# Delta-rule stage of a hybrid layer: the lower parts of its weights from GpSimd to VectorE

## The chip, the cores and the metric

The kernel runs on one core of a Trainium2 chip. Its engines are called by short names as the profile has them: PE is TensorE (matmuls; PEld its weight loads), DVE is VectorE, ACT is ScalarE, POOL is GpSimd, and SP is SyncE, which here only issues transfers. Each engine works through its own queue in order and waits on semaphores for the others. The metric is the device time of one execution in microseconds, given as the median of several runs.

## The reference, cut to what matters

One layer of a streaming encoder over 1024 positions and 1024 channels, in float32. One projection of the modulated input feeds two branches, a gated delta rule with 8 heads and a chunked band attention with 16; both are merged by gates, projected, normalised, and a convolved feed-forward part follows.

```python
h = x * (1.0 + scale_t) + shift_t
proj = h @ w_in[l]
qkv_a, z_a, beta_raw, a_raw, q_b, k_b, v_b, gates = jnp.split(proj, IN_SPLITS, axis=-1)
o_a = gated_deltanet(qkv_a, z_a, beta_raw, a_raw, conv_a[l], a_log[l], dt_bias[l], norm_a[l])
o_b = chunk_band_attention(...)
merged = gate_a * (o_a @ w_branch_a[l]) + gate_b * (o_b @ w_branch_b[l])
x = layernorm(DEEPNORM_ALPHA * x + gate_t * (merged @ w_o[l]), ln1_g[l], ln1_b[l])
...
x = layernorm(DEEPNORM_ALPHA * x + gate_f * ffn, ln2_g[l], ln2_b[l])
```

The delta rule of a head: q, k and v go through a causal convolution of width 4 and SiLU; for each chunk a lower triangular system is solved, and a state of 128x128 is carried from chunk to chunk.

## The kernel before, in words

**Split products.** Every large product of float32 matrices is done in three matmuls of a shorter format (fp32r). An operand `a` is split into a high part `ah`, its rounded copy, and a low part `al = a - ah`; the product is `ah*bh + ah*bl + al*bh`. The helper `split` (lines 175 to 180) makes both: the copy at line 177 (on ACT) or 179, the subtraction at line 180 on the engine `le`. `load_split` (line 182) loads a weight block of 128x1024 into a buffer `raw` through the SP queue (line 185) and splits it; `wblock` (line 274) allots the parts `wh` and `wl` and calls it, with ACT for the copy and POOL for the subtraction unless told otherwise. `raw`, `wh` and `wl` have three buffers each (`RB`, `WB`). `mm_fm` (line 280) does the matmuls of one half of 512 positions: 8 slices of 128 rows, three matmuls for each (line 284). A block is thus 48 matmuls, 16 of each of the three kinds.

**Order of the work.** The program is written stage by stage, head by head, but a planner lays the instructions of all engines out before the run, by a timing model of its own and by priorities (`tc.high_priority`), and only the order on each engine comes out of it. So the weight loads run some blocks ahead of their matmuls, and the dense products (TensorE's bulk) are placed between the small, dependent steps of the delta rule.

**The delta-rule stage** takes from about 80 to 800 us. For each of 8 heads there are:
- `stage_k`, `stage_q`, `stage_vz`: the projections of k, q, v and of the output gate z, one weight block each, fetched through the generator `halves` (line 511). `conv_in` (line 520) does the convolution of the projection: a first tap on ACT (line 526), three more on DVE (line 530, 0.74 us each), a tail of three columns added on DVE (line 540, both inputs in SBUF), then SiLU on ACT (line 541). `stage_k` ends with a product of 128x1024 on POOL (line 610), `stage_q` with another (line 636). `pk`, `pq` and `pv` are transposes of k, q and v on TensorE.
- `gate_block` (line 793): a block of the merge gates (`pgt`), also through `halves` (the first gate block, and k and q of head 0, take the products of the first blocks below instead); sixteen of these and two blocks of the attention's keys and queries (those that `EP` lists, through `qk_block`) serve as dense filling.
- `stage_solve` (line 656): 31 steps one after the other, each a product (line 663, both inputs in SBUF) and a reduce (line 665) on DVE; its result goes through DRAM (`ft_d`, from line 667) and back into the tile `dt_`, a part of group G.
- `stage_inverse`: starts with a transpose on DVE (line 682) and the product `pxt` on TensorE (line 687), then small steps over ACT, DVE, POOL and TensorE.
- `stage_chain` (line 716): eight steps of the state; in each, TensorE, DVE (`vs`, line 726, and the state, line 740), ACT (line 732) and TensorE take turns.
- `stage_out`, and `mod_rows` (line 803), which loads rows of another weight into `raw` buffers and sums them on DVE.

Three first blocks (`first_weights`) and the blocks of the later stages (`late_qk_block`, `qk_proj`, `v_proj`, the branch projections) call `wblock` directly, not through `halves`. In the tables the lower parts show as `wl<-raw,wh` at line 180 on POOL.

Of the kernel before, what the change touches and what calls it, by code (L numbers as in the profile page):

```python
# [12 lines left out]
ALU = mybir.AluOpType  # L13
# [4 lines left out]
P = 128  # L18
S = 1024
D = 1024  # L20
NK = 8
# [132 lines left out]
def hybrid_layer(  # L154
# [7 lines left out]
    PE, DVE, ACT, POOL, SP = nc.tensor, nc.vector, nc.scalar, nc.gpsimd, nc.sync  # L162
# [5 lines left out]
    def dump(key, src):  # L168
        if key in dbg:
            SP.dma_start(dbg[key], src)  # L170

    def f(ap):
        return ap.bitcast(F32)

    def split(h, l, src, he, le):
        if he is ACT:
            ACT.copy(h, src)  # L177
        else:
            he.tensor_copy(h, src)
        return le.tensor_tensor(l, src, f(h), ALU.subtract).ins  # L180

    def load_split(h, l, src, he, le, a=1):

        raw = W.tile([P, 1024], F32, tag="raw", bufs=RB, name=nm("raw"))
        SP.dma_start(raw.rearrange("p (a b) -> p a b", a=a) if a > 1 else raw, src)
        split(h, l, raw, he, le)

    def kview(w, c0, n):
        return w[:, c0:c0 + n].rearrange("(k p) n -> p k n", p=P)

    x2, out2 = x[0], out[0]
    w_ada2, w_in2 = w_ada[0], w_in[0]
# [31 lines left out]
    def nm(s):  # L224
        uid[0] += 1
        return f"{s}_{uid[0]}"
# [34 lines left out]
    def ring(key, shape, dtype=F32):  # L261
        return place(step(key, AT[key]), shape, dtype, key)
# [8 lines left out]
    def dhalf(name):  # L271
        return pbank(name, "d")

    def wblock(src, a, he=ACT, le=POOL):
        wh = W.tile([P, 1024], F32R, tag="wh", bufs=WB, name=nm("wh"))
        wl = W.tile([P, 1024], F32R, tag="wl", bufs=WB, name=nm("wl"))
        load_split(wh, wl, src, he, le, a)
        return (wh.rearrange("p (a b) -> p a b", a=a), wl.rearrange("p (a b) -> p a b", a=a))

    def mm_fm(ps, w, rh, rl, n, ks=range(NK)):  # L280
        wh, wl = w
        for k in ks:
            for a, r in ((wh, rh), (wh, rl), (wl, rh)):
                PE.matmul(ps, a[:, k, :], r[k][:, 512 * n:512 * n + 512],  # L284
                          start=(k == 0 and a is wh and r is rh),
                          stop=(k == NK - 1 and a is wl))
# [107 lines left out]
    for j in range(NK):  # L394
# [7 lines left out]
        for n in range(2):  # L402
            N = slice(512 * n, 512 * n + 512)
            px = pbank(nm("px"), "px")
            for t in range(4):
                tr = PE.transpose(px[:, t * P:t * P + P], xs[j][:, 4 * n + t, :], ident)
            ACT.activation(h32[:, N], px, AF.Identity, bias=cs[:, 0:1], scale=cs[:, 1:2])
            ACT.activation(hh[:, j, N], px, AF.Identity, bias=cs[:, 0:1], scale=cs[:, 1:2])
            POOL.tensor_tensor(hl[:, j, N], h32[:, N], f(hh[:, j, N]), ALU.subtract)
# [19 lines left out]
    for n in range(2):  # L429
        N = slice(512 * n, 512 * n + 512)  # L430
# [79 lines left out]

    def halves(name, col0, ready=None):

        w = None if ready else wblock(kview(w_in2, col0, P), NK)
        for n in range(2):
            ps = ready[n] if ready else dhalf(nm(name))
            if not ready:
                mm_fm(ps, w, hhk, hlk, n)
            yield n, slice(512 * n, 512 * n + 512), ps

    def conv_in(h, m):  # L520
        ti = m * NK + h
        y = big(f"y{m}")
        yf = flat(y)
        tail = sm("tail", 3)
        for n, N, ps in halves("pqkv", ti * P, pend.pop("qkv"[m], None) if h == 0 else None):
            ACT.activation(yf[:, N], ps, AF.Copy, scale=col("conv_a", 3 * 24 + ti))
            for tap in (2, 1, 0):
                d = 3 - tap
                o = yf[:, 512 * n + d:512 * n + 512]
                DVE.scalar_tensor_tensor(o, ps[:, :512 - d], col("conv_a", tap * 24 + ti), o,  # L530
                                         ALU.mult, ALU.add)
            if n == 0:

                DVE.tensor_scalar(tail, ps[:, 509:512], col("conv_a", ti), None, ALU.mult)
                for tap in (1, 2):
                    DVE.scalar_tensor_tensor(tail[:, 0:3 - tap], ps[:, 509 + tap:512],
                                             col("conv_a", tap * 24 + ti), tail[:, 0:3 - tap],
                                             ALU.mult, ALU.add)
            else:
                DVE.tensor_tensor(yf[:, 512:515], yf[:, 512:515], tail, ALU.add)  # L540
            ACT.activation(yf[:, N], yf[:, N], AF.Silu)
        return y
# [95 lines left out]
    def stage_vz(h, c):  # L638

        vT = conv_in(h, 2)  # L640
        if h == 0:
            dump("vT", flat(vT))
        vs = c["vs"] = big("vs")
        for g in range(2):
            pv = mbank("pv")
            for t in range(4):
                PE.transpose(pv[:, t, :], vT[:, 4 * g + t, :], ident)
            for t in range(4):
                u = 4 * g + t
                ACT.activation(vs[:, u, :], pv[:, t, :], AF.Copy, scale=c["bk"][:, u:u + 1])  # L650

        sz = c["sz"] = big("sz")
        for n, N, ps in halves("pz", 3 * D + h * P):
            ACT.activation(flat(sz)[:, N], ps, AF.Silu)
# [121 lines left out]
    def qk_block(i):  # L776

        for n, N, ps in halves("pqk", Q0 + i * P):
            gt_ = ring("gt", [P, 512])
            ACT.copy(gt_, ps)  # L780
            SP.dma_start(qk_d[i][:, N], gt_)
# [50 lines left out]
    def some_gates(n):  # L832
        for _, j in zip(range(n), gates):
            gate_block(j)
# [31 lines left out]
    for t in GE:  # L866
        with tc.issue_after(cs[-1]["steps"][t]):
            some_gates(1)


    def qk_proj(c0, p):
        if (c0 - Q0) // P + p in EP + LP:
            raw = W.tile([P, S], F32, tag="raw", bufs=RB, name=nm("raw"))
            SP.dma_start(raw, qk_d[(c0 - Q0) // P + p])
            for n in range(2):
                yield slice(512 * n, 512 * n + 512), raw[:, 512 * n:512 * n + 512]
            return
        w = wblock(kview(w_in2, c0 + p * P, P), NK)
        halves = []
        for n in range(2):  # L880
            ps = pbank(nm("pqk"), "qkv")
            for k in range(NK):
                for a, r in ((w[0], hh), (w[0], hl), (w[1], hh)):
                    PE.matmul(ps, a[:, k, :], r[:, k, 512 * n:512 * n + 512],
                              start=(k == 0 and a is w[0] and r is hh),
                              stop=(k == NK - 1 and a is w[1]))
            yield slice(512 * n, 512 * n + 512), ps

    def v_proj(g):
        w = [wblock(w_in2[4 * P * i:4 * P * i + 4 * P,  # L890
                          Q0 + 2 * D + 256 * g:Q0 + 2 * D + 256 * g + 256].rearrange(
                              "(k p) n -> p k n", p=P), 4) for i in range(2)]
        vts = [[ring("v", [P, 4, 2, P], F32R) for _ in range(2)] for _ in range(2)]
        for t in range(NT):
            ps = pbank(nm("pv"), "qkv")
            for k in range(NK):
                wh, wl = w[k // 4]
                for r, a in ((hh, wh), (hh, wl), (hl, wh)):
                    PE.matmul(ps[:, 0:256], r[:, k, t * P:t * P + P], a[:, k % 4, :],
                              start=(k == 0 and r is hh and a is wh),  # L900
                              stop=(k == NK - 1 and r is hl))
            for q in range(2):
                dst = vts[q][t // 4][:, t % 4]
                src = ps[:, P * q:P * q + P].rearrange("p (e d) -> p e d", e=2)
                ACT.copy(dst[:, :, 0:64], src)
                DVE.tensor_tensor(dst[:, :, 64:P], src, f(dst[:, :, 0:64]), ALU.subtract)
        return vts
# [127 lines left out]
    for br in range(2):  # L1035
# [4 lines left out]
        for j in range(NK):  # L1040
            w = wblock(kview(wbr[br], j * P, P), NK)
            for n in range(2):
                N = slice(512 * n, 512 * n + 512)
# [235 lines left out]
    for t in range(NT):  # L1279
# [5 lines left out]
        for n in range(2):  # L1285
            N = slice(512 * n, 512 * n + 512)
# [248 lines left out]
    for p in range(18, NP):  # L1535
        pair = []
        for i in range(2):
# [4 lines left out]
            h, l = (ring(o, [P, S], F32R) for o in ("lh", "ll"))  # L1542
# [99 lines left out]
```

## Time and profile before

| | |
|---|---|
| median of 3 runs | 2221.73 us (2216.29 to 2221.82) |
| the profiled execution | 2222.92 us |
| its span from first to last instruction | 2221.2 us |
| PE busy | 2125.3 us, 96% |
| DVE busy | 1555.7 us, 70% |
| ACT busy | 1037.9 us, 47% |
| POOL busy | 588.5 us, 26% |
| mean granted TensorE clock | 0.987 |
| PE, DVE, POOL busy from 80 to 800 us | 690.1, 493.1, 218.1 of 720 us |

How to read the profile's lines: a group of instructions is "line engine operation out<-in shape xcount | busy us, mean ns of one | idle time of the engine just before them, and what ended most of it". In a table of stretches the columns are the stretch, its length, the busy time of PE, PEld, DVE, ACT and POOL with the number of instructions, the granted TensorE clock, and the share and rate of the transfers. A line of waits reads "who, at which line, <- for whom: us in total, times, longest us". A line of a timeline is "start, duration, engine, line, operation, out<-in, shape, count". The names of tiles are those of the place in memory: FT holds the solve's result, G among others its coefficients and `dt_`, SA the state, SM small vectors.

### The profile page before, as it was taken

Reading aid. Unit: us, or ns where it says so; the run is one execution under the profiler, and the core shown is the slowest. Engines: PE = TensorE matmul, PEld = TensorE weight load, DVE = VectorE, ACT = ScalarE, POOL = GpSimd, SP = SyncE. Lnnn points to the kernel's source line nnn. Section 1 sums busy time; section 2 is a strip of 40 time slices with the busy share of each in tenths; the row PEclk is TensorE's granted clock in tenths of the full one; section 3 lists DMA queues with packets and bytes.
Section 4 is the critical chain, followed back from the end, with each engine's and each line's share of the span. In section 5 each row is a group of like instructions: output and inputs, shape, how many; then the busy total and the mean of one; then the engine's idle time right before and its main releaser. Section 6 shows DMA issues by size and latency. Waiting matters only on the chain. (4 is left out here: it accounts for less than half of the span.)

```text
span 2221.2 us, 31629 instructions
## 1 busy us (share of the span) xinstructions
PE 2125.3 (96%) x11469; PEld 1776.9 (80%) x11469; DVE 1555.7 (70%) x3228; ACT 1037.9 (47%) x2216; POOL 588.5 (26%) x544
## 2 busy tenths in 40 slices
PE   6998999999999999999999999999899999999998
PEld 5687787777878787798989788888788878887876
DVE  8567585765667664467676653556998788879897
ACT  4645253434334334467675642235544444445453
POOL 4323232332322232233342522424011000000023
PEclk9999999999999999999999999999999999999999
DMA  9232333423233412211111424342242222253222
GB/s 286 80 112 78 91 94 107 119 74 108 85 91 93 142 36 82 79 57 51 60 55 65 154 91 137 105 152 86 67 161 95 86 76 83 89 209 133 95 95 86
DMA packets 228415, 224.68 MB, mean 101 GB/s; under 512 B 27482, under 2 KB 184595, under 8 KB 228259
## 3 DMA queue, kind: packets, MB, share of 16 engines
q1 hardware_dynamic: 228179, 222.63, 31.6%
q8 instruction: 90, 1.47, 0.3%
q14 instruction: 66, 0.54, 0.1%
q10 hardware_dynamic: 80, 0.03, 0.0%
HBM read 180.63 MB, written 48.28 MB: 103 GB/s over the span
## 5 line engine op out<-in xcount | busy, mean ns | idle before, releaser
L180 POOL TENSOR_TENSOR wl<-raw,wh 128x1024 fp32r<-128x1024 f32 x88 | 212.2, 2413 | 325.4 <-ACT wh L177 303.1
L1193 PE MATMUL pup<-hh,wop 128*128 128x512 f32 x704 | 225.2, 391 | 1.6 <-DVE wop L180 1.6
L1193 PE MATMUL pup<-t,wop 128*128 128x512 f32 x792 | 190.1, 393 | 3.3 <-ACT t L177 2.0
L1193 PEld LDWEIGHTS pup<-t,wop 128*128 128x128 f32 x792 | 148.2, 188 | 38.0 <-ACT t L177 2.4
L1193 PEld LDWEIGHTS pup<-hh,wop 128*128 128x128 f32 x704 | 132.0, 188 | 31.0 <-DVE wop L180 2.0
L177 ACT CAST wh<-raw 128x1024 fp32r<-128x1024 f32 x88 | 92.4, 1050 | 134.6 <-DMA raw<-in_w_in_dram 56.0
L1234 POOL TENSOR_TENSOR cc<-cc,G 128x512 f32<-128x512 f32 x22 | 44.6, 2028 | 375.9 <-DVE G L1216 311.7
L284 PE MATMUL pqkv<-hh,wh 128*128 128x512 f32 x352 | 143.1, 407 | 0.0
L284 PE MATMUL pqkv<-hl,wh 128*128 128x512 f32 x352 | 140.8, 400 | 0.0
L284 PE MATMUL pqkv<-hh,wl 128*128 128x512 f32 x352 | 139.8, 399 | 0.0
L1193 PE MATMUL pup<-hl,wop 128*128 128x512 f32 x352 | 137.5, 391 | 0.0
L663 DVE TENSOR_TENSOR FT<-FT,G 128x16 f32<-128x16 f32 (+30 forms) x248 | 120.9, 488 | 17.6 <-POOL G L608 10.3
L944 POOL TENSOR_SCALAR G<-G,FT 128x640 f32<-128x640 f32 (+4 forms) x103 | 69.9, 681 | 182.3 <-DVE FT L943 160.4
L177 ACT CAST wop<-wr 128x512 fp32r<-128x512 f32 x110 | 65.6, 620 | 99.1 <-DVE wr L1179 65.1
L284 PE MATMUL pgt<-hh,wl 128*128 128x512 f32 x240 | 95.1, 396 | 0.8 <-POOL wl L180 0.8
L284 PE MATMUL pgt<-hh,wh 128*128 128x512 f32 x240 | 95.4, 397 | 0.3 <-DVE tmp L530 0.3
L284 PE MATMUL pgt<-hl,wh 128*128 128x512 f32 x240 | 94.7, 395 | 0.0
L1497 PE MATMUL pdn<-hl 128*128 128x512 f32 x360 | 86.7, 395 | 3.9 <-DVE hl L180 2.4
L180 DVE TENSOR_TENSOR wop<-wr,wop 128x512 fp32r<-128x512 f32 x110 | 80.2, 733 | 13.3 <-ACT wop L177 12.4
L963 DVE TENSOR_TENSOR pl<-pp,ph 128x512 fp32r<-128x512 f32 (+2 forms) x116 | 72.5, 635 | 17.4 <-ACT ph L962 16.6
L1497 PEld LDWEIGHTS pdn<-hl 128*128 128x128 f32 x360 | 68.5, 191 | 19.2 <-DVE hl L180 2.8
L941 ACT ACTIVATE G<-G,FT 128x640 f32<-128x640 f32 (+4 forms) x103 | 71.6, 696 | 19.0 <-DVE FT L936 16.9
(457 smaller groups left out, 6127.8 us busy)
## 6 DMA issues: line engine op xcount, KB each, us to landing
raw<-in_w_in_dram SPq DMA_DIRECT2D x72, 512.0 KB
wr<-in_w_up_dram SPq DMA_DIRECT2D x44, 512.0 KB
raw<-in_w_ada_dram SPq DMA_DIRECT2D x32, 512.0 KB
dr<-g_d SPq DMA_DIRECT2D x18, 512.0 KB
dr<-in_w_down_dram SPq DMA_DIRECT2D x18, 512.0 KB
wa<-in_w_ada_dram SPq DMA_DIRECT2D x32, 256.0 KB
gates_d<-GT SPq DMA_DIRECT2D x32, 256.0 KB
g_d<-G SPq DMA_DIRECT2D x14, 512.0 KB
```

Of the source, the lines that this page charges most:

```text
L177: ACT.copy(h, src)
L180: return le.tensor_tensor(l, src, f(h), ALU.subtract).ins
L284: PE.matmul(ps, a[:, k, :], r[k][:, 512 * n:512 * n + 512], start=(k == 0 and a is wh and r is rh), stop=(k == NK - 1 and a is wl))
L663: DVE.tensor_tensor(pr[:, :, 0:i + 1], ft[:, :, 0:i + 1], fa[:, i:i + 1, 0:i + 1].to_broadcast([P, 8, i + 1]), ALU.mult)
L941: ACT.activation(sb[:, 0:n], sb[:, 0:n], AF.Exp, bias=mx[:, nb - 1:nb], scale=-1.0, accum_out=mx[:, 2:3])
L944: POOL.tensor_scalar(sb[:, 0:n], sb[:, 0:n], mx[:, 3:4], 0.0, ALU.mult, ALU.add)
L963: DVE.tensor_tensor(pl[:, B, :], pp, f(ph[:, B, :]), ALU.subtract)
L1193: PE.matmul(ps, a[:, u, k, :], b[v][k], start=(new and k == 0 and u == 0 and v == 0), stop=(k == 3 and u == 1), skip_group_check=not new)
L1234: self.later(7, lambda: POOL.tensor_tensor(o, o, self.t, ADD))
L1497: PE.matmul(sets[s_][i], a[:, u, i * P:i * P + P], b[:, v, :], start=(new and not seed and j == 0 and u == 0 and v == 0), stop=(j == len(q ...
```

## The change

The generator `halves` asks `wblock` for the subtraction on DVE. `split` gets a branch: where the subtraction is on DVE, the source is 1024 wide and a flag `HS` is set, it is done as two instructions of 512 columns. The flag is set while the program up to the end of the delta-rule stage is written and cleared before the attention, so that later splits of that width on DVE stay whole. Nothing else is edited; the copy stays on ACT.

```diff
+    HS = [True]
+
...
             he.tensor_copy(h, src)
+        if le is DVE and src.shape[1:] == [1024] and HS[0]:
+            for n in range(2):
+                N = slice(512 * n, 512 * n + 512)
+                i = DVE.tensor_tensor(l[:, N], src[:, N], f(h)[:, N], ALU.subtract)
+            return i.ins
         return le.tensor_tensor(l, src, f(h), ALU.subtract).ins
...
     def halves(name, col0, ready=None):
 
-        w = None if ready else wblock(kview(w_in2, col0, P), NK)
+        w = None if ready else wblock(kview(w_in2, col0, P), NK, le=DVE)
...
         with tc.issue_after(cs[-1]["steps"][t]):
             some_gates(1)
 
+    HS[0] = False
```

## The prediction

> **What bounds the kernel now.** I began with the busy table and the table of stretches, cut so that the first stretch shown is the delta-rule stage, and then read who waits for whom on TensorE in it.
>
> ```profile
> PE 2125.3 (96%) x11469; PEld 1776.9 (80%) x11469; DVE 1555.7 (70%) x3228; ACT 1037.9 (47%) x2216; POOL 588.5 (26%) x544
> ...
> 80.00:800.00 720.00, 690.05 (x4066) 568.97 (x4065) 493.12 (x1220) 302.05 (x813) 218.07 (x203) 0.99 0.34 99
> ...
> 165.00:250.00 85.00, 79.16 (x505) 63.40 (x504) 60.09 (x148) 36.64 (x95) 27.94 (x36) 0.96 0.33 93
> ...
> 420.00:505.00 85.00, 78.14 (x476) 64.07 (x475) 56.43 (x135) 28.21 (x87) 24.65 (x26) 0.96 0.36 101
> ```
>
> TensorE is the bound of the whole kernel and of this stage: 690 of 720 us. The change takes no matmul away, so it can touch only the 30 us in which TensorE stands there, and the clock: two stretches of 85 us ran at a mean granted clock of 0.96, which is 0.04 x 85 = 3.4 us each. That ceiling, some 37 us or 1.7%, caps every gain below. What TensorE waits for, stage only:
>
> ```profile
> PE pxt L687 <- DMA G<-ft_d: 9.0, 9, 2.1
> PE pvn L729 <- DVE vs L726: 6.4, 8, 2.6
> PE pv L647 <- ACT pq L547: 3.0, 2, 2.3
> PE pk L572 <- ACT y L541: 2.8, 3, 1.5
> PE pu L735 <- ACT SA L732: 2.6, 5, 1.1
> ...
> PE pv L647 <- ACT tmp L541: 1.0, 1, 1.0
> PE pgt L284 <- POOL wl L180: 0.8, 1, 0.8
> ```
>
> Two things are to be seen. The operation that the change moves, the split wl on POOL, holds TensorE up once, for 0.8 us; so nothing is won by having the lower parts earlier. The largest wait is the first product of the inverse (pxt), which wants ft_d, the result of the row-by-row solve on DVE after its way through DRAM. Whatever shortens or lengthens the solve shows there.
>
> **What is removed.** Blocks whose weights change engine are those of the generator halves. Their number follows from the matmuls, 16 of each kind to a block:
>
> ```profile
> L284 PE MATMUL pqkv<-hh,wl 128*128 128x512 f32 x352 | 139.8, 399 | 0.0
> ...
> L284 PE MATMUL pgt<-hh,wl 128*128 128x512 f32 x240 | 95.1, 396 | 0.8 <-POOL wl L180 0.8
> ...
> L284 PE MATMUL pz<-hh,wl 128*128 128x512 f32 x128 | 51.8, 404 | 0.0
> ...
> L284 PE MATMUL pqk<-hh,wl 128*128 128x512 f32 x64 | 25.2, 393 | 0.0
> ```
>
> That is 22 + 15 + 8, and of the four pqk blocks the two that EP lists go through halves as well: 47. The next rows are what such a split costs POOL, and how it goes into a solve (DVE first, then POOL, the same four microseconds):
>
> ```profile
> L180 POOL TENSOR_TENSOR wl<-raw,wh 128x1024 fp32r<-128x1024 f32 x50 | 120.8, 2418 | 222.8 <-ACT wh L177 201.4 <-PE pgt L284 13.3 <-PE pfirst L284 4.3
> ...
> L636 POOL TENSOR_TENSOR y<-y,tmp 128x1024 f32<-128x1024 f32 x8 | 19.1, 2392 | 17.9 <-PE pq L630 13.8 <-ACT po L547 4.2
> L610 POOL TENSOR_TENSOR tmp<-tmp,SB 128x1024 f32<-128x1024 f32 x8 | 19.0, 2378 | 0.0
> ```
> ```profile
> 132.61 0.20 DVE L663 TENSOR_TENSOR FT<-FT,G 128x40 f32<-128x40 f32 x1
> 132.85 0.20 DVE L665 TENSOR_REDUCE FT<-FT 128x8 f32<-128x40 f32 x1
> 133.08 2.04 DVE L663 TENSOR_TENSOR FT<-FT,G 128x48 f32<-128x48 f32 x1
> 135.16 0.20 DVE L665 TENSOR_REDUCE FT<-FT 128x8 f32<-128x48 f32 x1
> 135.40 2.09 DVE L663 TENSOR_TENSOR FT<-FT,G 128x56 f32<-128x56 f32 x1
> ```
> ```profile
> 132.66 2.40 POOL L180 TENSOR_TENSOR wl<-raw,wh 128x1024 fp32r<-128x1024 f32 x1 [1.38 <-ACT wh L177]
> 135.01 2.40 POOL L636 TENSOR_TENSOR y<-y,tmp 128x1024 f32<-128x1024 f32 x1
> ```
>
> POOL loses 47 x 2.42 = 114 us of work, which by itself is worth nothing: POOL is a quarter busy. But a product of the solve, 0.20 us in the row before, takes 2.04 when it starts inside a POOL split, and ends as that split ends (135.12 and 135.06): it stands 1.84 us. How often, over all solves:
>
> ```profile
> L663 DVE TENSOR_TENSOR FT<-FT,G 128x16 f32<-128x16 f32 (+30 forms) x248 | 120.9, 488 | 17.6 <-POOL G L608 10.3
> ...
> L665 DVE TENSOR_REDUCE FT<-FT 128x8 f32<-128x16 f32 (+30 forms) x248 | 73.2, 295 | 6.9
> ```
>
> Product and reduce run over the same widths and take the same 0.20 us where nothing disturbs them, so the products stood for about 120.9 - 73.2 = 47.7 us. One POOL product of line 636 falls in each of the eight solves (it is issued by the query step just ahead) and takes 2.09 - 0.20 = 1.9 us of that, 15 in all, and stays. The other 32.5 us, 4.1 to a head, are some two splits per solve and go away.
>
> The Trainium skill, SBUF — State Buffer, section "Who interferes with whom", says that a VectorE instruction with two SBUF inputs and a GpSimd instruction that reads SBUF exclude each other for the whole of the instruction that came first. The rows above agree for the solve. By the same rule the new halves, which have two SBUF inputs, would in turn be caught by POOL's lines 636 and 610, which the rows do not show for lack of halves. From the rows' times that catch would be (19.1 + 19.0) / 720 = 5% of 94 halves at some 1.2 us each, 6 us more on DVE and at most one on TensorE: the sum below would be -6 instead of -7. I go by the rows of the next part and leave that microsecond to the range.
>
> **What is added.** DVE gets 94 subtractions of 128x512, both inputs in SBUF. The stage has none; the later stages have both widths on DVE (minimum, median, maximum in ns):
>
> ```profile
> L180 DVE TENSOR_TENSOR wop<-wr,wop x110: 670/683/1619, 1460.7 to 1960.2; 128x512 fp32r<-128x512 f32 x110
> ...
> L180 DVE TENSOR_TENSOR ob<-raw,ob x6: 1216/1224/1226, 1279.4 to 1358.2; 128x1024 fp32r<-128x1024 f32 x6
> ```
>
> At 0.683 us that is 64 us. Two halves cost 1.37 against 1.22 for one whole, 7 us over 47 blocks, for which other work may slip between them. DVE in the stage goes from 493 to 493 - 32.5 + 64 = 525 us or 73%: not a bound. What counts is where the halves fall.
>
> In a solve: the two splits that lay inside now put 2 x 1.37 = 2.7 us, with gaps 2.8, between its steps. The solve ends 4.1 - 2.8 = 1.3 us earlier; 4.1 if the planner sets the halves outside. The nine pxt waits sum to 9.0 us, mean 1.0. A cut of 1.3 removes all but the tails of the longest: I take 6.5 us, with bounds 0 (the planner moves pxt forward by as much) and 9.0.
>
> In the convolutions: line 540 is a DVE addition of two SBUF tiles three columns wide, and ACT's SiLU waits behind it.
>
> ```profile
> L540 DVE TENSOR_TENSOR y<-y,SM x16: 145/153/2381, 83.4 to 772.5; 128x3 f32<-128x3 f32 x16
> ...
> ACT y L541 <- DVE y L540: 39.4, 15, 5.5
> ```
>
> Its median is 0.15 us and its longest 2.38, nearly a whole POOL operation. Of the 2.8 + 1.0 us that TensorE waits behind that SiLU I take 1.5, bounds 0 and 3.8. The clock: the two stretches with 0.96 are those in which TensorE idles most, 5.8 and 6.9 us of 85 (from their rows); with waits cut I take 1.5 of the 6.8 us, bounds 0 and 6.8.
>
> In the chain: halves fill 64 / 720 = 9% of DVE's time. A state update of lines 726 or 740 that comes up finds one running 9 times in 100, with 0.34 us left on average, 0.03 us per update; some hundred updates make 3 us on DVE. TensorE has dense blocks to cover most of it; waits for vs were 6.4 us in all. I take 1.0, bounds 0 and 3.
>
> A new wait: the half stands in DVE's in-order queue until ACT's cast of the same block is done. Behind it stand the solve, the convolution taps and the chain's updates, and behind those ACT and TensorE. POOL stood 201 us for such casts at no cost. The next rows are ACT's waits for raw loads, DVE's own halves in the up-projection, and DVE's and SP's waits around the solve:
>
> ```profile
> ACT wh L177 <- DMA raw<-in_w_in_dram: 43.1, 8, 10.8
> ...
> L180 DVE TENSOR_TENSOR wop<-wr,wop 128x512 fp32r<-128x512 f32 x88 | 64.5, 736 | 8.5 <-ACT wop L177 7.9
> ...
> DVE G L682 <- DMA G<-ft_d: 12.0, 4, 8.1
> ...
> SPq L185 <- POOL wl L180: 95.0, 18, 14.2
> ```
>
> By the up-projection, where 88 halves stood 7.9 us in all for their casts, it is 0.09 us a half, 8 us over 94; by ACT's own waits for raw loads, behind which its casts stand, it is 43. The first is the nearer row, since the planner orders both queues. On TensorE I take 1.5, bounds 0 and 15 (worked out under the rivals). The SP queue waits 95 us for splits to free the raw buffer ahead of the next load; the end of a split moves from cast + 2.4 to cast + 1.4 us plus a place in DVE's queue, so I count nothing there. The cover for all lateness of wl is the ring of three buffers: each block is 48 matmuls, so a split has two blocks of time before its reader; if DVE were late by more than that, every microsecond would show on TensorE.
>
> **Sum.** -6.5 - 1.5 - 1.5 + 1.0 + 1.5 = -7.0 us on the profiled execution, which took 2222.92 us (span 2221.2): 2215.9. The median of the runs, 2221.73, lies 1.2 us under it, so I forecast 2214.7, with 2207 to 2219 if this mechanism decides.
>
> **Rivals.** No change: TensorE is 96% busy, the planner lays out all queues anew with the longer DVE work in its books, and puts pxt and the chain so that the same waits come back in other places. What DVE gains in freed products (32.5 us) is half of what it takes on (64), which speaks for this; that pxt waits in most heads for what the plan cannot know speaks against. It gives 2219 to 2224, say 2221.7. The Trainium skill, Perfetto Trace Analysis, section "Optimizing Scalar/DVE Operations", warns in this sense that moving work between GpSimd and VectorE might not help because they share a read port.
>
> Slower: DVE stands at a half for a late cast. The place is just behind each solve: the raw load is issued in the SP queue behind the ft_d transfers, ACT has waited there eight times, 43.1 us in all. DVE would stand with it, and has stood 12.0 us there anyway for ft_d: 31 us new, on the inverse and the first chain steps. If half reaches TensorE, that is +15, and with half of the gain of 7 left, +12: 2234. It decides from the point where the planner places the halves ahead of the inverse's operations in DVE's queue. Against it: that same planner knows that load and its place.
>
> Not what it says: if the shape test at the new branch fails, each block is one subtraction of 1.22 us; DVE saves 7 us, a solve is held in longer pieces, and I expect about 2216 to 2220, a little short of the forecast.
>
> **Chances.** Forecast 0.45, no change 0.27, slower by the cast 0.23, whole subtractions 0.05, which I count as no change. A measurement of this kernel can tell about 0.3%, 6.7 us, from nothing. Faster by more than that 0.45, within it 0.32, slower 0.23. The range takes in the forecast's bounds and most of the slow rival: 2203 to 2234.
>
> **What would show it.** Right: no product of line 663 over 1 us except one per solve (line 636), its mean near 0.36 us; 94 halves at about 0.69 us on DVE between 80 and 800 us; the pxt waits under 4 us; DVE near 525 us there. Wrong: DVE idle before line 180 for ACT's cast of wh in tens of microseconds, with more waits of TensorE for vs or the inverse; or the same 30 us of TensorE's idle time under other names; or a different time in stages after 800 us, which the edit leaves alone except through the planner's order.

## The result and the profile after

The changed kernel took 2230.48 us (median of its runs, 2222.08 to 2240.98) against 2221.20 for the kernel before, a ratio of 1.0043 [1.0032, 1.0054]: 0.43% or some 9.3 us slower, where 7 us faster had been forecast. Its profiled execution took 2233.22 us (span 2231.5), 10.3 more than that of before. Line numbers are 2 to 8 higher in it: the cast is line 179, the split 187, pxt 694, vs 733.

The row for all engines, from the page, and then the delta-rule stage in the table of stretches:

```profile
PE 2136.4 (96%) x11469; PEld 1782.8 (80%) x11469; DVE 1566.4 (70%) x3275; ACT 1033.0 (46%) x2214; POOL 470.9 (21%) x497
```
```profile
80.00:800.00 720.00, 691.46 (x4015) 567.12 (x4014) 496.19 (x1242) 294.37 (x801) 101.31 (x155) 0.98 0.34 99
```

POOL has lost its work (218 to 101 us in the stage), and DVE has hardly more than before (493 to 496). DVE has 47 instructions more in all, 3228 to 3275, and not 94. The groups of DVE say why, and what became of the solve:

```profile
L670 DVE TENSOR_TENSOR FT<-FT,G 128x16 f32<-128x16 f32 (+30 forms) x248 | 93.3, 376 | 14.8 <-POOL G L615 8.1
...
L672 DVE TENSOR_REDUCE FT<-FT 128x8 f32<-128x16 f32 (+30 forms) x248 | 73.2, 295 | 7.0
...
L187 DVE TENSOR_TENSOR wl<-raw,wh 128x1024 fp32r<-128x1024 f32 x47 | 59.9, 1274 | 46.6 <-ACT wh L179 46.3
```

The 47 blocks are whole subtractions of 128x1024: the branch for halves is never taken, because `src.shape[1:]` is a tuple and a tuple never equals the list `[1024]`. What ran is thus the kernel before with nothing but `le=DVE` in `halves`. And the last column has a wait that the kernel before does not have on this engine: 46.3 us before the split, until ACT's cast of the same block. The waits of the stage, first TensorE's and then those of DVE and ACT (who, at which line, for whom: us, times, longest):

```profile
PE pvn L736 <- DVE vs L733: 8.1, 10, 2.6
PE pu L742 <- ACT SA L739: 5.9, 5, 2.0
PE pk L579 <- ACT y L548: 4.1, 5, 2.0
...
PE pks L732 <- DVE SA L747: 2.0, 2, 1.7
...
PE pxt L694 <- DMA G<-ft_d: 0.7, 2, 0.5
```
```profile
DVE wl L187 <- ACT wh L179: 46.3, 24, 5.0
...
ACT wh L179 <- DMA raw<-in_w_in_dram: 41.7, 8, 7.5
```

The pxt waits are nearly gone (9.0 to 0.7 us), as forecast. In their place the waits of the chain and of SiLU have grown: vs 6.4 to 8.1, SA on ACT 2.6 to 5.9, y 2.8 to 4.1, SA on DVE 0.4 to 2.0. DVE's wait for casts is about as long as ACT's own wait for the raw loads behind which the casts stand. One place shows how they hang together. Behind the solve of the seventh head, DVE, then ACT, TensorE and the SP queue:

```profile
738.98 1.30 DVE L689 STREAM_TRANSPOSE G<-G 128x512 f32<-128x512 f32 x2 [2.44 <-DMA G<-ft_d]
740.21 1.49 DVE L825 SCALAR_TENSOR_TENSOR GT<-raw,csil,GT 128x512 f32<-128x512 f32 x2
743.15 1.23 DVE L187 TENSOR_TENSOR wl<-raw,wh 128x1024 fp32r<-128x1024 f32 x1 [1.44 <-ACT wh L179]
744.29 0.34 DVE L733 SCALAR_TENSOR_TENSOR vs<-pks,SM,vs 128x128 f32<-128x128 f32 x1
744.66 0.29 DVE L697 TENSOR_SCALAR G<-pxt 32x128 f32<-32x128 f32 x1
```
```profile
742.07 1.04 ACT L179 CAST wh<-raw 128x1024 fp32r<-128x1024 f32 x1 [5.87 <-DMA raw<-in_w_in_dram]
```
```profile
740.57 0.38 PE L732 MATMUL pks<-SA,y 128*128 128x128 f32 x2
...
744.78 0.64 PE L736 MATMUL pvn<-vs,am 128*128 128x128 f32 x2 [2.56 <-DVE vs L733]
```
```profile
734.81 2.75 SPq L677 DMA_DIRECT2D G<-ft_d  x4
...
738.11 1.17 SPq L192 DMA_DIRECT2D raw<-in_w_in_dram  x2
```

The raw load of v's block is issued behind the solve's transfers (738.11, behind 734.81). So ACT casts it only at 742.07. DVE's queue has the split of that block between the transposes of the inverse (line 689) and everything that follows. It stands 1.44 us and then works for 1.23; the update vs, ready long before (its product pks ran at 740.57), starts at 744.29, and TensorE has stood 2.56 us. The same stands behind six solves (at 255.0, 353.9, 448.3, 553.4, 648.0 and 743.2 us), with waits of 1.4 to 2.8 us, 13.8 together. Other splits, with waits of their own, lie inside the solves: fourteen in all, with 17.1 us of work and 11.8 us of standing. So a solve gets no shorter by the freed products: the eight took 30.1 us on average before and 30.2 after, that of the seventh head 29.2 us in both profiles (691.6 to 720.7 before, 701.6 to 730.8 after). A solve in the third head:

```profile
324.46 0.29 DVE L670 TENSOR_TENSOR FT<-FT,G 128x128 f32<-128x128 f32 x1
...
326.52 1.22 DVE L187 TENSOR_TENSOR wl<-raw,wh 128x1024 fp32r<-128x1024 f32 x1 [1.77 <-ACT wh L179]
327.67 0.28 DVE L672 TENSOR_REDUCE FT<-FT 128x8 f32<-128x128 f32 x1
```

**Idle time and clock.** Summed over the whole profile from the records of TensorE and of its clock, TensorE stood 80.6 us before and 79.7 after, from its first matmul to its last: no more than before. What grew in these two executions is the time at half clock: 11 windows of together 51.2 us before, 16 of 68.3 us after. Half of what TensorE worked in them is lost, 23.2 and 31.9 us; the 8.7 us between these are most of the 10.3. The mean clocks agree: (0.987 - 0.983) x 2231 = 9 us. Over all executions the clock weighs less. Its mean is 0.9855 in the 22 of the changed kernel, and 0.9866 in 77 of the kernel before on the chips of the experiments: 0.0011 x 2230 = some 2.5 of the 9.3 us. The profiled execution is one of the slower ones. The other 7 us are not in the clock, and the profiled pair doesn't show where they lie. The windows begin where gaps lie. Behind the place shown above:

```profile
740.00:744.00 4.00, 2.22 (x25) 1.47 (x23) 2.52 (x4) 1.21 (x2) 0.96 (x4) 1.00 1.07 303
744.00:748.00 4.00, 3.22 (x35) 2.74 (x36) 1.84 (x6) 0.91 (x5) 0.00 (x0) 0.62 0.60 201
```

The granted clock (third column from the end) falls from 1.00 to 0.62 just as TensorE goes on. In these two executions nearly the same sum of idle time thus cost more clock than before. The gaps are not fewer: 75 of over 0.2 us in both, and 24 before and 26 after of over 1 us.

### The profile page after: what moved, and what is told of

It reads as the page before. It is cut to its first block, busy times and chain, and to the rows that moved or that the text cites. A ratio compares the mean times of both kernels' runs of the same rounds, so it can differ in the third digit from the quotient of the medians.

```text
span 2231.5 us, 31652 instructions
## 1 busy us (share of the span) xinstructions
PE 2136.4 (96%) x11469; PEld 1782.8 (80%) x11469; DVE 1566.4 (70%) x3275; ACT 1033.0 (46%) x2214; POOL 470.9 (21%) x497
## 4 chain that ended last, share of the span: by engine, by line
PE 42%; DVE 6%; issue 2%; ACT 1%; DMA 1%; POOL 1%; DVEq 0%; SPq 0%; ACTq 0%; POOLq 0%
PE pup L1201 17%; PE pbr L1055 8%; PE pwo L1117 4%; PE pdn L1505 4%; PE pqk L892 2%; PE pv L907 2%; PE po L982 2%; PE pp L967 1%; PE ps L941 1%; DVE hl L187 1%; DVE hh L1593 1%; DMA dr<-g_d 0%; DVE hh L1519 0%; ACT hh L1588 0%; PE pn L1316 0%
## 5 line engine op out<-in xcount | busy, mean ns | idle before, releaser
L187 POOL TENSOR_TENSOR wl<-raw,wh 128x1024 fp32r<-128x1024 f32 x41 | 98.4, 2402 | 117.6 <-ACT wh L179 111.7
L670 DVE TENSOR_TENSOR FT<-FT,G 128x16 f32<-128x16 f32 (+30 forms) x248 | 93.3, 376 | 14.8 <-POOL G L615 8.1
L187 DVE TENSOR_TENSOR wl<-raw,wh 128x1024 fp32r<-128x1024 f32 x47 | 59.9, 1274 | 46.6 <-ACT wh L179 46.3
L971 DVE TENSOR_TENSOR pl<-pp,ph 128x512 fp32r<-128x512 f32 (+2 forms) x116 | 72.5, 635 | 17.1 <-ACT ph L970 16.2
```

Source lines behind the costliest of these rows:

```text
L670: DVE.tensor_tensor(pr[:, :, 0:i + 1], ft[:, :, 0:i + 1], fa[:, i:i + 1, 0:i + 1].to_broadcast([P, 8, i + 1]), ALU.mult)
L971: DVE.tensor_tensor(pl[:, B, :], pp, f(ph[:, B, :]), ALU.subtract)
```

## The experiments

The theory to be tested, called A in the expectations: the loss is DVE's wait, in order, for ACT's late casts, above all that of v just behind each solve. The rivals put it on the whole subtractions in place of halves, on the operations of DVE and POOL that catch each other, or on the planner's new order of everything. That last one needs a caution for every run: where blocks change engine or place, the planner lays out all queues anew. In the changed kernel at least 1075 of TensorE's 11469 matmuls stand in another order than before (so many have to be left out of both traces for the rest to agree; this count is given below for the other runs). Two pairs were therefore made in which no other instruction moves. Ratios are to the kernel before on the same chip (medians 2219.9 to 2220.2 us).

**The halves made true.** The shape test mended, so that the change does what its diff says.

```diff
-        if le is DVE and src.shape[1:] == [1024] and HS[0]:
+        if le is DVE and tuple(src.shape[1:]) == (1024,) and HS[0]:
```

> The shape test mended, so that each of the 47 subtractions is really made as two of 128x512 on VectorE (0.68 us each). Theory A (VectorE stands in its in-order queue for a late cast, above all for the v block's, whose raw load is issued behind ft_d): the waits for the cast stay, 40 to 55 us on VectorE, and the time stays slower than before by 6 to 12 us. Rival B (sheer load: every block moved costs its share of the 9 to 10 us): 7 us more work on VectorE, so slower by 10 to 12 us. Rival C (the planner's new order happens to be a worse one, whatever the subtractions do): anything between -5 and +12 us, with gaps of TensorE in other places than in the changed kernel.

2227.51 us, 1.0031 [1.0021, 1.0041]. Still slower, perhaps by a little less: the intervals overlap.

```profile
L180 DVE TENSOR_TENSOR wl<-raw,wh x94: 669/684/3246, 81.8 to 766.4; 128x512 fp32r<-128x512 f32 x94
```
```profile
DVE wl L180 <- ACT wh L177: 41.1, 22, 4.8
```

There are 94 halves of 0.68 us, as the prediction priced them, and the wait for casts stays: 41.1 us. That the halves weren't made explains at most a small part.

**v's blocks back on POOL, the other 39 on DVE; and the reverse.**

```diff
-    def halves(name, col0, ready=None):
+    def halves(name, col0, ready=None, le=DVE):
...
-        w = None if ready else wblock(kview(w_in2, col0, P), NK)
+        w = None if ready else wblock(kview(w_in2, col0, P), NK, le=le)
...
-        for n, N, ps in halves("pqkv", ..., ...):
+        for n, N, ps in halves("pqkv", ..., ..., POOL if m == 2 else DVE):
```

The second kernel has `le=POOL` in the first line and `DVE if m == 2 else POOL` in the last.

> As the changed kernel, but the 8 v blocks (one per head, 7 or 8 loads just behind ft_d) keep their subtraction on GpSimd; 39 stay on VectorE. Theory A: VectorE no longer stands before the inverse and the chain; the gaps of TensorE just behind each solve (five of 1.0 to 2.5 us, with half clock after most) go, and with them 5 to 9 us: within 4 us of the kernel before. Rival B: 39/47 of the loss stays, slower by about 8 us. Rival C: anything.

> The kernel before, with only the 8 v blocks moved to VectorE. Theory A: VectorE stands some 2 us for the cast in most heads, 12 to 20 us in all, TensorE shows gaps behind the solves; slower by 4 to 9 us although only a sixth of the blocks is moved. Rival B: a sixth of the loss, slower by 1.6 us. Rival C: anything.

Without v: 2222.94 us, 1.0016 [1.0006, 1.0027]. v alone: 2229.44 us, 1.0043 [1.0029, 1.0057]. DVE's wait with v alone, and then the products of the solve in the other kernel:

```profile
DVE wl L180 <- ACT wh L177: 15.0, 7, 2.8
```
```profile
L663 DVE TENSOR_TENSOR FT<-FT,G 128x16 f32<-128x16 f32 (+30 forms) x248 | 94.1, 379 | 16.9 <-POOL G L608 10.3
```

Eight blocks of 47 bring as much as the whole loss, 9.6 us, with 15.0 us of wait on DVE, and here only 63 of TensorE's matmuls moved. They also bring DVE eight subtractions of 1.2 us, so this run alone doesn't part the wait from the work. The other 39 bring the freed products (94.1 us against 120.9) and no gain: they come out a little slower than before, with 23.3 us of wait for casts left on DVE.

**Halves on POOL.** The same blocks stay on POOL, in two pieces each (`HS` set around `wblock` in `halves`).

> The subtractions stay on GpSimd, but the 47 are made in two halves of 512. No VectorE wait for a cast is possible and no VectorE work is added; only the planner sees other instructions, and GpSimd holds VectorE's products for about 1.2 us at a time instead of 2.4. Theory A and rival B: within 4 us of the kernel before. Rival C: a new order alone can move the time by 5 us or more, either way.

2218.66 us, 0.9986 [0.9974, 0.9998]: at most a hair faster, with 82 matmuls moved. The products of the solve took 112.1 us, 8.8 less than before. On POOL the size of a piece matters little.

**The wait alone.** No instruction moves. For each of v's eight blocks DVE copies one column of the cast (0.15 us), and so has to wait for it (`look` is `m == 2`). The order of TensorE, ACT, POOL and SP is that of the kernel before, instruction for instruction, and DVE's but for the eight copies.

```diff
+    prb = cst.tile([P, 1], F32, tag="prb", name="prb")
...
         w = None if ready else wblock(kview(w_in2, col0, P), NK)
+        look and DVE.tensor_copy(prb, f(w[0][:, 0, 0:1]))
```

> The kernel before with all subtractions on GpSimd; for each of the 8 v blocks VectorE gets one copy of a single column of the cast part wh (about 0.06 to 0.2 us of work), which does nothing but make it stand in its queue until ACT's cast is done. Theory A: VectorE stands 10 to 20 us for casts in all, and the time is slower by 4 to 9 us with hardly any work added. Rival B: within 2 us of the kernel before.

2233.53 us, 1.0060 [1.0047, 1.0073], 13.4 us slower, where 4 to 9 had been expected. DVE's waits, one place in its timeline, and TensorE's waits:

```profile
DVE prb L513 <- ACT wh L177: 16.1, 7, 3.3
```
```profile
740.54 0.15 DVE L513 COPY prb<-wh 128x1 f32<-128x1 f32 x1 [2.31 <-ACT wh L177]
740.72 0.35 DVE L726 SCALAR_TENSOR_TENSOR vs<-pks,SM,vs 128x128 f32<-128x128 f32 x1
```
```profile
PE pxt L687 <- DMA G<-ft_d: 10.8, 9, 2.5
PE pvn L729 <- DVE vs L726: 9.3, 10, 1.9
```

The eight copies of together 1.2 us do no work worth the name, free no product (121.1 us) and change no order, and DVE stood at them seven times, 16.1 us in all, with vs and the inverse behind it. But not all of the 13.4 us is this wait. The new tile `prb` changes something else: the opening, before the first copy runs at 86.5 us without having to wait. The first 40 us of the kernel before and of this one, and the last products of the opening in the same order (first and last start):

```profile
0.00:40.00 40.00, 22.44 (x99) 18.03 (x99) 30.31 (x48) 16.60 (x30) 20.21 (x26) 1.00 1.00 292
0.00:40.00 40.00, 20.42 (x91) 16.78 (x92) 26.96 (x42) 15.04 (x28) 19.68 (x25) 1.00 1.01 252
```
```profile
L284 PE MATMUL pfirst<-hh,wl x48: 387/390/628, 23.0 to 79.7; 128*128 128x512 f32 x48
L284 PE MATMUL pfirst<-hh,wl x48: 387/393/628, 24.0 to 84.2; 128*128 128x512 f32 x48
```

The transfers run at 252 GB/s instead of 292, and TensorE ends the opening 4.5 us late. The three kernels of this study that have the tile (this one and two further down) all show it, with 252 to 254 GB/s; the eleven without it have 285 to 293. Whether the place of the other tiles in memory does it was not tested. Matmul by matmul, TensorE here is 4.5 us late at 85 us and 11.7 at 808 us, so 7.2 us come in the stage of the copies; its idle time from 80 to 830 us rose from 30.0 to 35.8. Over its five executions the mean clock is 0.9864, against 0.9867 for the kernel before on this chip, so hardly any of the loss is clock. The 13.4 us less the 4.5 leave an estimate of some 9 us for the wait, close to the 9.6 of v's blocks alone. That supports the mechanism of theory A without the planner, with a price of about 9.

**v's split later in DVE's queue.** If the place is what costs, v's blocks should be harmless on DVE behind the inverse. `issue_after` ties them behind its last copy (line 714). `conv_in` hands over `late`, `inv[-1] if m == 2 else None`. Once only v is on DVE (`le`), and once all 47 blocks.

```diff
+    inv = [None]
...
-            DVE.tensor_copy(am[lo_, G, hi_], pT[lo_, :, lo_])
+            inv.append(DVE.tensor_copy(am[lo_, G, hi_], pT[lo_, :, lo_]).ins)
...
+        with tc.issue_after(late) if late else nullcontext():
             w = None if ready else wblock(kview(w_in2, col0, P), NK, le=le)
```

> As the kernel with the 8 v blocks alone on VectorE, with the same 8 subtractions of 1.22 us, but each is tied in VectorE's queue behind the last VectorE step of the inverse (line 714), some 10 us later, when the cast is long done. The work on VectorE is the same, only the wait for the cast ahead of the inverse and the chain is gone. Theory A (the wait does it): the loss of 9 us goes, within 3 us of the kernel before; VectorE waits under 2 us for casts. Rival B (the work does it): slower by 7 to 10 us as with the v blocks alone.

> All 47 subtractions whole on VectorE as in the changed kernel, the 8 of the v blocks tied behind the last step of the inverse. Theory A: as with v on GpSimd and the other 39 on VectorE, slower than before by 2 to 5 us. Rival B: as the changed kernel, slower by 9 to 10 us.

Only v: 2237.45 us, 1.0080 [1.0064, 1.0095], the slowest kernel of all. All 47: 2207.52 us, **0.9941 [0.9929, 0.9953]**, 13 us faster than before and the best of the study. Both miss what theory A expected, one on each side. In the slow one DVE has no wait for casts any more. TensorE's largest wait there:

```profile
PE pxt L687 <- DMA G<-ft_d: 14.0, 8, 5.3
```

The planner moved 762 of TensorE's matmuls there. POOL still has the blocks of k, q and the gates, and three of its splits fall into each of three solves, which take 32 to 33 us (before into one): the products sum to 124.8 us. pxt is late by 14.0 us instead of 9.0. That accounts for 5 us of the 17. In its profiled execution TensorE stood 9.6 us longer than before and lost 7.8 us more to the clock; why was not followed up. A new plan may thus cost more than the wait does. The best version, TensorE's waits, then DVE's, then the same place behind a solve on DVE and on ACT:

```profile
PE pvn L729 <- DVE vs L726: 5.1, 8, 2.2
PE pu L735 <- ACT SA L732: 4.6, 6, 1.1
PE pk L572 <- ACT y L541: 2.9, 4, 0.9
```
```profile
DVE wl L180 <- ACT wh L177: 27.9, 14, 4.7
```
```profile
721.85 1.30 DVE L682 STREAM_TRANSPOSE G<-G 128x512 f32<-128x512 f32 x2 [2.42 <-DMA G<-ft_d]
723.08 1.50 DVE L818 SCALAR_TENSOR_TENSOR GT<-raw,csil,GT 128x512 f32<-128x512 f32 x2
724.49 0.34 DVE L740 SCALAR_TENSOR_TENSOR SA<-SA,SM,pu 128x128 f32<-128x128 f32 x1
724.87 0.29 DVE L690 TENSOR_SCALAR G<-pxt 32x128 f32<-32x128 f32 x1
```
```profile
723.49 1.05 ACT L177 CAST wh<-raw 128x1024 fp32r<-128x1024 f32 x1 [4.41 <-DMA raw<-in_w_in_dram]
```

The cast comes just as late (723.49, behind 4.41 us of waiting on ACT), and on DVE nothing stands behind it: the state and the inverse go on at once. TensorE stood 71.5 us in all and lost 15.9 to the clock (7 windows), against 80.6 and 23.2 before: 9.1 + 7.3 = 16.4 us, all of the 15.4 between the two profiled executions.

**The wait put back into the best version.** To the last kernel the eight one-column copies are added, at v's former place. The order of all other engines is the same, instruction for instruction.

```diff
         with tc.issue_after(late) if late else nullcontext():
             w = None if ready else wblock(kview(w_in2, col0, P), NK, le=le)
+        look and DVE.tensor_copy(prb, f(w[0][:, 0, 0:1]))
```

> As the kernel with all 47 on VectorE and v tied behind the inverse (12.7 us faster than before), plus one copy of a single column of the v block's wh on VectorE at the place where the split used to stand; the order on all other engines is the same, instruction for instruction. Theory A: the wait alone gives back most of the gain, 6 to 14 us, so between 7 us faster than before and equal to it. Rival C (the gain and the loss are the planner's other order): the order is the same, so the time stays 12 us faster than before.

2219.37 us, 0.9997 [0.9986, 1.0007]: 11.9 us back (the best version ran on another chip, where the kernel before took 2220.17 us against 2220.14 here). DVE's waits, with the new one second:

```profile
DVE wl L180 <- ACT wh L177: 27.8, 14, 4.7
...
DVE prb L514 <- ACT wh L177: 12.4, 6, 3.3
```

DVE stands 12.4 us more. But this kernel has the tile `prb` too, and its TensorE is already 5.6 us late at 85 us, before the first copy; that leaves an estimate of some 6 us for the wait. In the profiled pair even that isn't seen in the stage: TensorE's idle time from 80 to 830 us rose by 2.6 us only (21.1 to 23.7), and most of the delay came behind 830 us, where the clock took 14.9 us instead of 7.5. So this run doesn't show that the wait alone takes the whole gain away. The other 27.8 us of waits for casts are there in both kernels, and the best version has its gain in spite of them: the sum of the waits on DVE doesn't decide.

**The exclusion put back into the best version.** POOL does k's and q's subtractions a second time, with the same values into the same tile (14 instructions; `again` is `m < 2`), and so blocks products of the solve as before. The matmuls of those blocks then depend on POOL too, and 292 of TensorE's matmuls moved against the best version.

```diff
-        split(h, l, raw, he, le)
+        RAW.append(raw); split(h, l, raw, he, le)
...
+        again and w and POOL.tensor_tensor(w[1].rearrange('p a b -> p (a b)'), RAW[-1],
+            f(w[0].rearrange('p a b -> p (a b)')), ALU.subtract)
```

> As the kernel with all 47 on VectorE and v tied behind the inverse, plus the old cost: for the k and q blocks of heads 1 to 7 GpSimd does the same subtraction a second time into the same wl (14 operations of 2.4 us, which fall into the solves). Theory A with the prediction's first term: two products per solve stand about 1.9 us again, pxt waits come back to 4 us or more, and the time is 4 to 9 us slower than without the repeats. If the freed products were worth nothing on TensorE: within 3 us of the kernel without them.

2231.09 us, 1.0049 [1.0037, 1.0061], 23.6 us slower than the best version, where 4 to 9 had been expected. The products and TensorE's waits:

```profile
L664 DVE TENSOR_TENSOR FT<-FT,G 128x16 f32<-128x16 f32 (+30 forms) x248 | 108.9, 439 | 14.3 <-POOL G L609 7.6
```
```profile
PE pxt L688 <- DMA G<-ft_d: 7.9, 4, 4.2
PE pks L726 <- DVE SA L741: 7.7, 5, 3.9
```

The pxt waits are back (7.9 us), and new waits of the chain for DVE beside them. POOL's operations at these places hurt, more than the prediction's 6.5 us. How much of it is products of the solve (the eight took 32.1 us on average, against 30.1), how much other DVE work caught by POOL and how much the other order, this run doesn't part.

**The exclusion taken away alone.** From the kernel before: everything stays on POOL, but k's and q's splits for the next head are tied behind the solve's last step, by a small copy on POOL of its result.

```diff
+        sol.append(POOL.tensor_copy(prb, ft[:, 7, 31:32]).ins)
...
+        with tc.issue_after(late) if late else nullcontext():
             w = None if ready else wblock(kview(w_in2, col0, P), NK)
...
+        ..., sol[-1] if m < 2 else None):
```

> All subtractions on GpSimd, but those of the k and q blocks of the next head, the two that fall into a solve, are tied in GpSimd's queue behind a copy of one column that waits for the solve's last step. So no split holds up a product of the solve, and VectorE gets no work and no wait. Theory A with the prediction's first term (a solve that is 3 to 4 us shorter takes away most of the 9 us of waits for pxt): products of the solve sum to about 93 us instead of 121, pxt waits under 3 us, faster by 4 to 9 us. If the term is worth nothing (TensorE's idle time only moves elsewhere): within 3 us of before, or slower by what a later k or q block costs.

2222.17 us, 1.0014 [1.0005, 1.0022], no gain, although the products fell to 98.0 us, the solves to 26.8 us on average and the pxt waits to a third:

```profile
PE pxt L688 <- DMA G<-ft_d: 3.3, 4, 1.6
...
PE pqkv L284 <- POOL wl L180: 2.7, 1, 2.7
```

A new wait of 2.7 us for the later split takes back half of the 5.7, and 455 matmuls moved. This kernel is also the third with the tile `prb`: its last product of the opening starts at 86.0 us, 6.3 later than before. Less these, it would be some 4 us faster than before (an estimate: 2.0 slower less 6.3), so what shorter solves are worth by themselves stays open here.

**Two variants of the best version.** All blocks tied, k and q behind the solve and v behind the inverse; and the best version with the mended shape test, so with true halves.

```diff
-            DVE.tensor_reduce(ft[:, :, i:i + 1], ...)
+            last_ = DVE.tensor_reduce(ft[:, :, i:i + 1], ...)
+        sol.append(last_.ins)
...
-        ..., inv[-1] if m == 2 else None):
+        ..., inv[-1] if m == 2 else sol[-1]):
```

> As the kernel with all 47 on VectorE and v tied behind the inverse, and the k and q subtractions of the next head tied behind the solve's last step, so that a solve holds neither their work nor their waits (1.9 us each time). Theory A: the solve is 4 to 5 us shorter again and VectorE's waits for casts fall from 28 to under 15 us; 10 to 20 us faster than before. If k's later release of its raw buffer holds up the loads: 0 to 8 us faster than before.

> As the kernel with all 47 on VectorE and v tied behind the inverse, with each subtraction made in two halves of 512 as the change's words say. Theory A: the wait decides and not the width, so within 5 us of the kernel with whole ones, 7 to 15 us faster than before.

All tied: 2223.29 us, 1.0013 [1.0001, 1.0026]; 10 to 20 us faster had been expected. DVE's waits for casts are the shortest of all kernels with 47 blocks there, 12.1 us, but one late split holds TensorE itself:

```profile
PE pqkv L284 <- DVE wl L180: 5.2, 1, 5.2
```

With true halves: 2215.94 us, 0.9979 [0.9967, 0.9991], 8 us slower than with whole subtractions, where at most 5 had been expected. Twice as many instructions bring nothing in this place; the plan is another one again (395 matmuls moved against the best version), so the 8 us are not put down to the halves alone.

## Why the prediction was wrong

**The step that failed** is the price of the new wait. The prediction saw it, named what is queued behind it, and had two rows for it: 8 us on DVE by the up-projection, 43 by ACT's waits for raw loads. It chose "The first is the nearer row, since the planner orders both queues" and took 1.5 us on TensorE. The far row was the right one: DVE stood 46.3 us, ACT 41.7. That one planner orders both queues did not bring the cast in time, since the cast itself stands for a load that is issued behind the solve's transfers. The nearer row was the one that waits for the same loads, not the one with the same instruction. Against the 1.5 us forecast, v's waits alone cost some 9 us in the kernel before (an estimate: the copies, less the slower opening; v's blocks alone cost 9.6), inside the bound of 15 that the prediction gave.

**The slower rival** had the place ("just behind each solve"), the cause (the raw load issued behind ft_d) and the point from which it decides (the planner places the split ahead of the inverse's operations in DVE's queue); all three are in the timeline at 743 us. Its price was +12 us, measured +9.3. That the price came out near is partly luck: it took 31 us of new standing on DVE behind the solves with half of it on TensorE, while the six stands there sum to 13.8 us, and the rest of the 46.3 lies in other places. It had a chance of 0.23. The measured time lies in the stated range, 2203 to 2234, only because that range had taken in this rival.

**Freed products: right in size, wrong in worth.** 32.5 us forecast, 120.9 - 93.3 = 27.6 measured; pxt waits cut by 8.3 us, 6.5 forecast. The second agreement is luck, because the step that was to bring it, "The solve ends 1.3 us earlier", didn't come: the solves last as long as before, since splits with their waits now lie inside. What changed is TensorE's side. Its first pxt started 5.1 to 8.0 us after the end of a solve before (6.4 on average) and 7.3 to 10.5 after (9.2), so it came later and had less to wait for; the planner, which now has the splits in its plan of the solve, may be the reason, but that was not tested. By the Trainium skill, SBUF — State Buffer, section "Who interferes with whom", this exclusion had to go, and the trace agrees. That rule's other half, POOL catching the new operations, was put at 6 us; measured is 59.9 - 47 x 1.224 = 2.4 us, nearly all of it in one split of 3.78 us. And a wait of TensorE that goes is not time won. With v on POOL the pxt waits were down to 1.0 us and the kernel was not faster: TensorE stood 79.1 us in all, against 80.6.

**SiLU behind line 540.** The blocked tails went as thought (10.0 + 2.8 us before, 6.1 + 1.2 after), yet TensorE's waits behind that SiLU grew from 3.8 to 4.1 + 1.9 = 6.0 us, where 1.5 less was forecast.

**Clock.** 1.5 us of gain forecast; a loss of 8.7 measured in the profiled execution and of some 2.5 over all executions. The sum assumed that the clock follows the sum of idle time; in the profiled pair that sum stayed the same and the loss grew.

**The subtractions in front of the chain** were put at 1.0 us with a bound of 3: vs waits grew by 1.7, the cast waits included.

**DVE's load** came to 496 us in the stretch from 80 to 800, not 525; the stage now ends 9 us later (the last pks starts at 926.9 instead of 918.2), so the stretch holds less of it. DVE was also freed elsewhere, which the prediction left out: the eight small products of line 583 (both inputs in SBUF) fell from 7.5 to 1.3 us. DVE's total is no bound in any of the kernels.

**Not what it says.** This rival had a chance of 0.05, and it is true; its price (a little short of the forecast) fell with the forecast. Mended, the change is still slower than before.

**What makes the best version.** Not shown. It gets slower again with the wait put back (some 6 us besides the opening, same order) and with POOL's subtractions put back (23.6 us, another order). But the kernel with v on POOL has neither v's wait on DVE nor the blocked products, and it is 15 us slower than the best version. So the rival of the planner's order stands for the gain: 1045 of TensorE's matmuls moved against the kernel before, and the near variants came out between 2216 and 2237 us. The Trainium skill, Perfetto Trace Analysis, section "Optimizing Scalar/DVE Operations", says that moving work between GpSimd and VectorE might not help, since they share a read port; here the move hurt by 0.43% as written, through a wait more than through the port (only 2.4 us of splits caught on DVE), and came out 0.59% faster with eight of the 47 blocks in another place.

## What to carry to other kernels

When an operation moves from an engine with little to do to a busy one that works in order, its price is first what it waits for and who stands behind it there, and only then its work: POOL's 201 us of idling before the split was this warning. Take the duration of the new wait from whoever waits for the same event now, not from the same instruction elsewhere; a tiny instruction that does nothing but wait, put into an otherwise unchanged order, measures it, once you have seen that the parts ahead of it take as long as before. If the wait is real, try the operation later in the queue before giving up the move (here one such try won 13 us and another lost 17), and expect a removed wait to be worth nothing until TensorE's whole idle time and its clock have been summed again. One profiled execution is not the median: look at the clock of all executions before putting a loss down to it.

## What the runs showed of the hardware

TensorE's clock went to half behind short gaps. In the changed kernel gaps of 2.0 us (at 179.7), 1.9 (210.3), 1.4 (352.8), 1.0 (447.6), 2.0 (622.0), 2.0 (670.2) and 2.6 us (742.2) were each followed by windows at half clock of 3.4 or 6.8 us. Behind the gap at 352.8 us:

```profile
354.00:358.00 4.00, 2.91 (x35) 2.19 (x36) 2.67 (x6) 0.97 (x6) 0.00 (x0) 0.73 0.62 180
358.00:362.00 4.00, 4.00 (x24) 3.54 (x24) 0.84 (x3) 1.19 (x5) 0.31 (x1) 0.50 0.03 8
```

In the second row TensorE is busy throughout and still at 0.50. The Trainium skill, TensorE: Matmul & The Clock Gate, section "HAM oscillation — how this bites in real kernels", gives as its rule no idle gaps over some 3.4 us. The length of the windows agrees with that figure; the gaps here were all shorter, and the measurement decides: in small dependent steps, with other short gaps around it, one of 1.0 to 2.6 us can be enough. It need not be: a gap of 1.7 us at 610.4 in the same trace was followed by no window, and the same gap of 1.9 us at 63.8 was followed by one in the changed kernel and by none in the kernel before. Which property of a gap decides was not tested. Executions of one kernel differ by the clock as well: the fastest of the changed kernel, 2222.08 us, ran at 0.989, and the slowest, 2240.98, at 0.980, and 0.009 x 2230 = 20 us is all of the 19 between them. The gaps at 622 and 670 us stand in the kernel without v on DVE too, and not in the best version; they come with the plan, and are not shown to be the wait's.
